# Layer with attention and experts on one core: zeros on ScalarE, the last gate's modulation in the attention stage, another order in the routing

## The chip, the cores and the metric

The kernel runs on one core of a Trainium2 chip. A core has five engines that run their own instruction queues and wait for each other through semaphores: TensorE (PE, matmuls), VectorE (DVE), ScalarE (ACT), GpSimd (POOL) and SyncE (SP, which here issues the large DMA transfers). The metric is the device time of one execution in microseconds.

## The reference

One layer over 512 tokens of width 1024, float32. A conditioning vector c gives six modulations (shift, scale and gate, twice).

```python
cond = silu(c)
mod = cond @ ada_w[l] + ada_b[l]
sh1, sc1, gt1, sh2, sc2, gt2 = split(mod, 6)
h = _ln(x) * (1 + sc1) + sh1
parts = split(h @ w_in[l])                 # one projection, three mixers
y = concat([mla(...), window(...), nsa(...)]) @ w_out[l]
x = layernorm(ALPHA * x + (1 + gt1) * y)
h = _ln(x) * (1 + sc2) + sh2
scores = sigmoid(h @ router_w); biased = scores + router_bias
# pick 1 of 4 groups of experts by its best two, then 2 of its 4 experts;
# weights are the two scores, normalised
g, u = h @ w_gate[e], h @ w_up[e]          # per expert, 1024 -> 256
y = sum over chosen e of weight * ((silu(g) * u) @ w_down[e])
x = layernorm(ALPHA * x + (1 + gt2) * y)
```

`gt2`, the last gate, is needed only at the very end of the expert stage.

## The kernel before, in words

The 512 tokens are four blocks of 128 (n = 0 to 3). The stages in order of time: modulations and input projection; MLA, sliding window and NSA attention by token block, interleaved by hand in the string `ORD` (`q` queries, `n` NSA of a token block, `s` modulation steps, `g` steps of the last gate's modulation, `o` output projection, `Z` and `L` mark where buffers change hands); output projection of a block with its layernorm; routing of that block; experts. The order on each engine comes from a planner that lists instructions by priority, with offsets in the table `PRM` and a few forced places (`issue_after`, `together`).

A modulation step (`mod_half`) loads four weight tiles `ada`, multiplies them with the conditioning vector in 16 matmuls into `modps` (two `gemv` of 8) and adds the result in two VectorE adds. `gstep` is that of gate 2. In the `ORD` of before no `g` stands, so its two steps run where `step(16, gsteps)` is written, after the last output projection, and `gate_out(1, m3)` adds one and writes the gate to DRAM, from where `gate_in` reads it back for all partitions. Weight tiles `ada`, the output weights' `wo20` to `wo31`, the gates and the gather targets `x1g` share five buffers of a pool (`wraw`).

The output weights of the last two parts are split into a high part `woh` (a cast on ScalarE) and a low part `wol` (a subtraction on GpSimd).

Routing (`route(n, ...)`): transposes of the normalized rows (`x1p`, copied to `x1T`), logits `lps`, their sum `lsum`, the router's function `th`, affinities `aff`, biased scores `bia`, group sums `gs`, choice of group and experts (`asg`), ranks by matmuls (`rkp`), one-hot operands (`rh`, `r`, `rg`), and tables by matmuls: `tabp` gives `tokB`, the token indices of the gathers, `tabq` the weights and output places. Then `prep(q)` gathers the rows of an expert group's row blocks (`rows`), block b=0 from the first two token blocks alone (`xsA_d`), b=1 and 2 from all (`xs_d`); they are transposed (`gTp`) and evicted with scale and shift on ScalarE (`gT`). Gathers skip missing rows, so their targets are zeroed first.

Experts: four groups q of four experts. For each group eight steps k of gate/up matmuls (`gu`), each for three row blocks b, then `silu`, product, transposes `atp`, down projection `dn`, and combination. `warm` matmuls of no use to the result keep TensorE's clock up during the routing. The small tables `tokh` and `cmxp` are needed for the output's indices and for a count of overflowing rows.

## Time and profile before

| what | us |
|---|---|
| median of 3 runs | 593.4 (591.91 to 599.62) |
| the profiled execution | 596.7 |
| its span, first to last instruction | 594.8 |
| attention of token blocks 2 and 3, with output projection of blocks 0 and 1 | about 255 to 346 |
| rest of the output projection, routing of blocks 0 to 2 | 346 to 384.6 |
| routing of block 3, first expert block | 384.6 to 427.4 |
| experts, to the end of the span | 427.4 to 594.8 |

Times in the trace count from the start of the span. A row gives an instruction or a run of like ones; "idle before" with an arrow names who ended an engine's wait. The mean granted TensorE clock of the execution was 0.965 of full speed.

### The profile page before, as it was taken

The page shows a single profiled execution, that of the slowest core. Times are in us where ns is not written, and L with a number is a line of the kernel's source. Part 1 is how long each engine was busy: PE and PEld are TensorE (multiplying, and loading weights), DVE is VectorE, ACT ScalarE, POOL GpSimd, SP SyncE. Part 2 cuts the span into 40 slices and gives each one's busy share as a digit, 9 for nine tenths or more (in the row PEclk, how much of TensorE's full clock was granted, in tenths as well). Part 3 has the DMA queues.
Part 4 walks back from the last instruction along what each step waited for, and adds up shares of the span by engine and source line. Part 5 has one row for each costly group of instructions (what it writes and reads, how often), then busy time and mean ns, then how long its engine had stood idle before and what let it go on. Part 6 is the DMA issues. An engine that isn't in the chain of part 4 may idle for free.

```text
span 594.8 us, 10444 instructions
## 1 busy us (share of the span) xinstructions
PE 548.7 (92%) x3856; PEld 333.1 (56%) x3856; DVE 368.2 (62%) x1219; ACT 222.1 (37%) x556; POOL 97.4 (16%) x114
## 2 busy tenths in 40 slices
PE   2899999999899999999899999978899999999990
PEld 1559775687788998755455456653434234234240
DVE  7515656664678568877769568886138157167174
ACT  2514443561428336374634512121434062070130
POOL 0114200000010010003301112123502122011022
PEclk9969999999799999999999999978999999999996
DMA  8993246743930200098300685359699999999601
GB/s 301 373 328 108 83 142 225 260 153 102 323 91 19 72 37 1 2 220 226 124 2 0 222 278 200 119 209 306 164 370 351 366 365 348 374 356 354 248 1 47
DMA packets 77546, 117.05 MB, mean 197 GB/s; under 512 B 7937, under 2 KB 54440, under 8 KB 77492
## 3 DMA queue, kind: packets, MB, share of 16 engines
q1 hardware_dynamic: 72328, 102.60, 52.9%
q0 software_dynamic: 4960, 13.64, 6.3%
q8 instruction: 32, 0.52, 0.4%
q14 instruction: 22, 0.18, 0.1%
q10 hardware_dynamic: 204, 0.11, 0.1%
HBM read 112.12 MB, written 8.40 MB: 203 GB/s over the span
## 4 chain that ended last, share of the span: by engine, by line
PE 78%; DVE 11%; issue 3%; DMA 3%; ACT 2%; POOL 2%; ACTq 0%; POOLq 0%
PE gu L1319 13%; PE zps L407 13%; PE dn L1370 7%; PE onsa L894 6%; PE yps L1215 5%; PE zall L423 3%; PE modps L323 2%; PE modps L375 2%; PE gTp L997 2%; PE cmb L1410 2%; PE stp L501 2%; PE sps L921 2%; PE wps L849 1%; PE warm L356 1%; PE cmh L1418 1%
## 5 line engine op out<-in xcount | busy, mean ns | idle before, releaser
L1319 PE MATMUL gu<-gu,gT 128*32 128x512 f32 x768 | 85.3, 596 | 0.1
L1319 PEld LDWEIGHTS gu<-gu,gT 128*32 128x32 f32 x768 | 23.8, 110 | 52.5 <-issue 50.6
L1370 PE MATMUL dn<-dn,aT 128*32 128x512 f32 x384 | 45.3, 597 | 0.4 <-ACT aT L127 0.2
L1343 DVE TENSOR_TENSOR act<-act,gu 128x256 f32<-128x256 f32 x12 | 5.1, 421 | 59.8 <-ACT act L1342 59.8
L1002 ACT ACTIVATE gT<-gTp,modc,modc 128x128 f32<-128x128 f32 x96 | 35.7, 461 | 10.1 <-PE gTp L997 9.5
L1342 ACT ACTIVATE act<-gu 128x256 f32<-128x256 f32 x12 | 4.6, 387 | 72.1 <-PE gu L1319 72.1
L1215 PE MATMUL yps<-wol,oM 128*128 128x512 f32 x64 | 30.9, 595 | 0.0
L1375 DVE SCALAR_TENSOR_TENSOR y<-dn,tab,gt 128x512 f32<-128x512 f32 x24 | 18.0, 748 | 10.2 <-PE dn L1370 10.2
L323 PE MATMUL modps<-ada,cond 128*32 128x512 f32 x128 | 18.3, 631 | 4.4 <-DVE gr L1079 4.1
L1370 PEld LDWEIGHTS dn<-dn,aT 128*32 128x32 f32 x384 | 10.4, 109 | 20.8 <-issue 18.5
L894 PE MATMUL onsa<-pt,vs 128*64 128x512 f32 x40 | 20.6, 614 | 0.0
L491 ACT ACTIVATE Sg<-Sg,nms 128x128 f32<-128x128 f32 (+3 forms) x32 | 17.8, 559 | 3.7 <-DVE nms L490 3.3
L491 ACT ACTIVATE W<-W,nmw 128x256 f32<-128x256 f32 (+1 forms) x32 | 15.3, 478 | 9.7 <-DVE nmw L490 9.3
L997 PEld LDWEIGHTS gTp<-cf,rows 128*128 128x128 f32 x96 | 10.4, 142 | 15.1 <-ACT gT L1002 9.2
L448 DVE TENSOR_TENSOR rp<-zps,trig 128x128 f32<-128x128 f32 (+1 forms) x28 | 9.7, 345 | 12.9 <-PE zps L407 12.5
L356 PE MATMUL warm<-cf 128*128 128x128 f32 x88 | 17.2, 326 | 0.1
L407 PE MATMUL zps<-B1s,hH 128*128 128x256 f32 x64 | 15.1, 329 | 2.2 <-DVE B1s L210 1.1
L356 PEld LDWEIGHTS warm<-cf 128*128 128x128 f32 x88 | 13.8, 222 | 5.5 <-issue 4.7
L1378 DVE TENSOR_TENSOR ys<-y,ys 128x512 fp32r<-128x512 f32 x22 | 15.2, 692 | 2.1 <-ACT ys L127 1.4
L997 PE MATMUL gTp<-cf,rows 128*128 128x128 f32 x96 | 14.8, 282 | 1.6 <-DMA rows<-xs_d,tokB 1.6
L127 ACT COPY pt<-stp 128x512 f32<-128x512 f32 x14 | 7.9, 586 | 22.2 <-PE stp L501 21.9
L1389 ACT ACTIVATE R<-R,rsf 128x1024 f32<-128x1024 f32 x3 | 3.7, 1241 | 31.4 <-DVE rsf L1388 31.4
...
## 6 DMA issues: line engine op xcount, KB each, us to landing
...
```

The costliest lines, as they stand in the source:

```text
L323: return lambda: PE.matmul(ps[32 * j:32 * j + 32], cond[:, k], t[:, 512 * (j % 2):512 * (j % 2) + 512], start=first, stop=last, skip_group ...
L356: PE.matmul(ps[:, :128], ident, ident, start=True, stop=True)
L407: PE.matmul(ps[:, :w], l[:, k, ts_], get(k, r), start=(k == 0 and i == 0), stop=(k == KD - 1 and i == 2))
L423: m = PE.matmul(outs[n], l[:, k, n * 128:(n + 1) * 128], get(k, r), start=(beg and n % 2 == 0), stop=(k == KD - 1 and i == 2), skip_group_ ...
L491: S.activation(S_h, S_h, AF.Exp, bias=nm, scale=-1.0, accum_out=den)
L894: PE.matmul(ops[64 * g:64 * g + 64, cols], lhsT, rhs, start=first[g], stop=False, skip_group_check=True)
L997: PE.transpose(ps[:, k * 128:(k + 1) * 128], src[:, (4 * a + k) * 128:(4 * a + k + 1) * 128], ident)
L1002: S.activation(dst[:, kk], pk, AF.Identity, bias=sh2(kk), scale=sc2(kk))
L1215: last = PE.matmul(ps, l, r[:, cs], start=(i == 0), stop=(i == len(order) - 1))
L1319: together([lambda e=e: PE.matmul(gu[b][32 * e:32 * e + 32], gT[b][:, k, 32 * e:32 * e + 32], w[:, e], start=(k == 0), stop=(k == KD - 1), ...
L1370: together([lambda b=b, e=e, f=f: PE.matmul(dn[b][32 * e:32 * e + 32], aT[b][:, f, 32 * e:32 * e + 32], wd[f][:, e], start=(f == 0), stop= ...
L1375: V.scalar_tensor_tensor(y, dn[b], tab[:, s:s + 1], gt2[:, cs], op0=OP.mult, op1=OP.mult)
```

## The change

Four edits. The six buffers that gathers write into (`rows1`, `rows2`, four `x1g`) are zeroed by ScalarE, as a product with zero, instead of GpSimd memsets. The last gate's modulation gets two places `g1` in `ORD`, around the NSA attention of block 2, with priority offset -40. The copies of `x1T` go to ScalarE (which they did) and the pass that writes `t` is listed behind the last of them. The gate/up steps k=3 to 7 of the first expert group are listed behind `tabq` of the last token block.

```diff
@@ -21,9 +21,9 @@
 PRM = {
     "A0": -40, "A1": -300, "A2": 150, "A3": 300, "LA0": -300, "LA1": -40, "LA2": 600, "LA3": -300,
     "NW": [6, 2, 3, 5], "ORA": "k0 k1 k2 l0 l1 l2 l3 k3",
-    "ORD": "q0 q1 n0 n1 q2 q3 s1 n2 Z n3 o0 s2 s1 s2 o1 o2 s2 o3 L", "SWb": 2, "WF": 2, "aTe": "S", "c10": -600,
+    "ORD": "q0 q1 n0 n1 q2 q3 s1 g1 n2 g1 Z n3 o0 o1 o2 o3 L", "SWb": 2, "WF": 2, "aTe": "S", "c10": -600,
     "c11": -40, "c12": -300, "c13": -600, "cpt": "S", "evatp": "S", "evbtp": "SVSV", "evstp": "SSV", "evwtp": "VS",
-    "gst1": 80, "gst2": 40, "kndE": "V", "lTe": "V", "mg": -300, "mh0": 300, "mh2": 20, "mla1": 20, "mla2": 80,
+    "gst1": -40, "kndE": "V", "lTe": "V", "mg": -300, "mh0": 300, "mh2": 20, "mla1": 20, "mla2": 80,
     "mq0": 600, "mq2": 80, "mq3": 150, "mskE": "VG", "mskb": 3, "nl0": 20, "nl1": 150, "nl2": 300, "nl3": 600,
     "np0": -150, "np2": 600, "np3": -80, "ns1": -40, "ns2": 20, "ns3": -40, "nsa1": -20, "nsa3": 600, "nv0": -300,
     "nv1": -20, "nv3": 150, "nw0": 300, "nw1": 600, "nw2": 150, "nw3": -80, "oM": "S", "oNc": "S", "oS": "S",
@@ -39,7 +39,7 @@
     "wB0": 2, "wB1": 3, "wB3": 1, "wK5": 1, "wL3": 2, "wM": 1, "wR0": 4, "wR2": 4, "wR3": 6, "wT2": 2, "wT3": 4,
     "wY31": 4, "wo0": -80, "wo1": 300, "wo2": -300, "wo20": 80, "wo21": -600, "wo3": 150, "wo30": 150,
     "wo31": -600, "woE": "GG", "wohE": "S", "ws0": 4, "ws1": 1, "ws3": 1, "wz0": 1, "wz3": 2, "wzf0": 1,
-    "x1T": "SS", "x1bk": "tq", "ybk": "z", "yhi": "V", "yhi3": "S", "ylo": "V", "ylo3": "VG", "yxb": 4, "zrb": 5,
+    "x1bk": "tq", "ybk": "z", "yhi": "V", "yhi3": "S", "ylo": "V", "ylo3": "VG", "yxb": 4, "zrb": 5,
 }
 T, D, NT, KD = 512, 1024, 4, 8
 NEG = -1.0e30
@@ -937,7 +937,17 @@
                 with pri(f[t[0]][1] + t[1]):
                     f[t[0]][0](int(t[1]))
 
-        outproj = gstep = None
+        gsteps = []
+
+        def gstep(n):
+
+            if not gsteps:
+                step(16)
+                gsteps.extend((mod_bias(10, 2), 0))
+                gsteps[1] = mod_half(gsteps[0], 1)
+            step(n, gsteps[1])
+
+        outproj = None
         ORD = pr("ORD", "q0 n0 q1 n1 s1 q2 q3 Z n2 n3 L o0 o1 o2 g1 o3 g1")
         partA, partB = ORD.split("Z")
         partB, partC = partB.split("L")
@@ -970,12 +980,6 @@
                 load_wo(a, b, wol[a][:, b])
         gt1 = wraw("gt1")
         gate_in(0, gt1)
-        m3 = mod_bias(10, 2)
-        gsteps = mod_half(m3, 1)
-
-        def gstep(n):
-            step(n, gsteps)
-
         for a in range(WF, 4):
             for b in range(2):
                 raw = wraw(f"wo{a}{b}")
@@ -1055,6 +1059,7 @@
             V.memset(g8[n], BIGF)
             V.memset(t8[n], BIGF)
         base = rp.tile([128, 20], F32, name="base")
+        tabq = []
 
         def route(n, lps, rs):
             def r_(name, *shape):
@@ -1162,7 +1167,8 @@
             for kk in range(2):
                 PE.matmul(tq[:, 0:2 * NSLOT], ohp[:, kk], r2[:, kk].rearrange("p a c -> p (a c)"), start=(kk == 0),
                           stop=False, skip_group_check=True)
-            warm(f"wT{n}", PE.matmul(tq[:, 2 * NSLOT:2 * NSLOT + 8], ohg, rg, start=False, stop=True, skip_group_check=True))
+            tabq.append(PE.matmul(tq[:, 2 * NSLOT:2 * NSLOT + 8], ohg, rg, start=False, stop=True, skip_group_check=True))
+            warm(f"wT{n}", tabq[-1])
             V.tensor_tensor(tab[:, NSLOT:], tab[:, NSLOT:], tq[:, 0:TW - NSLOT], op=OP.add)
             if n == NT - 1:
                 V.tensor_copy(tokG, tab[:, 3 * NSLOT:])
@@ -1229,13 +1235,14 @@
                     ps = bank(pick("x1bk", "t", hf), "x1p")
                     for k in range(4):
                         PE.transpose(ps[:, k * 128:(k + 1) * 128], x1[:, (4 * hf + k) * 128:(4 * hf + k + 1) * 128], ident)
-                    cp(pick("x1T", "SS", hf), x1T[:, 4 * hf:4 * hf + 4], heads(ps, 4))
+                    x1c = S.copy(x1T[:, 4 * hf:4 * hf + 4], heads(ps, 4))
                     V.bn_stats(st[:, hf], x1[:, cs])
             G.dma_start(x1_d[n * 128:(n + 1) * 128], x1)
             fin()
             nm = yp.tile([128, 1], F32, name="ynm", bufs=2)
             V.scalar_tensor_tensor(nm, mv2[:, 0:1], -1.0, rs2, op0=OP.mult, op1=OP.mult)
-            S.activation(t2, x1, AF.Identity, bias=nm, scale=rs2)
+            with tc.issue_after(x1c.ins):
+                S.activation(t2, x1, AF.Identity, bias=nm, scale=rs2)
             for d_ in (xsA_d, xs_d)[n >= 2:]:
                 G.dma_start(d_[n * 128:(n + 1) * 128], t2)
 
@@ -1268,11 +1275,15 @@
         ep = pool(est, "ep", 2, side="right")
         wst2 = pool(est, "wst2", NW2, side="right")
         rows_ += [ep.tile([128, D], F32, name=f"rows{i}", bufs=1) for i in range(1, NROW)]
+        def zero(dst):
+
+            S.mul(dst, cf[:, :dst.shape[-1]], 0.0)
+
         for r in rows_[1:]:
-            G.memset(r, 0.0)
+            zero(r)
         cnt_w = [0]
-        step(16, gsteps)
-        gate_out(1, m3)
+        gstep(16)
+        gate_out(1, gsteps[0])
         gt2 = wraw("gt2")
         gate_in(1, gt2)
         lg2 = ep.tile([128, D], F32, name="lg2", bufs=1)
@@ -1315,17 +1326,19 @@
                 for u, nm in enumerate(("moe_w_gate", "moe_w_up")):
                     SP.dma_start(w[:, :, 256 * u:256 * u + 256],
                                  A[nm][4 * q:4 * q + 4, k * 128:(k + 1) * 128].rearrange("e p f -> p e f"))
-                for b in range(CAPB):
-                    together([lambda e=e: PE.matmul(gu[b][32 * e:32 * e + 32], gT[b][:, k, 32 * e:32 * e + 32], w[:, e],
-                                                    start=(k == 0), stop=(k == KD - 1), skip_group_check=True)
-                              for e in range(4)])
+
+                with tc.issue_after(tabq[-1].ins) if q == 0 and k >= 3 else nullcontext():
+                    for b in range(CAPB):
+                        together([lambda e=e: PE.matmul(
+                            gu[b][32 * e:32 * e + 32], gT[b][:, k, 32 * e:32 * e + 32], w[:, e],
+                            start=(k == 0), stop=(k == KD - 1), skip_group_check=True) for e in range(4)])
             if pending:
                 pending.pop()()
             with pri("mg"):
                 x1g, x2g = x1g_[2 * (q % 2)], x1g_[2 * (q % 2) + 1][:, 0:512]
                 if q < 2:
-                    G.memset(x1g, 0.0)
-                    G.memset(x2g, 0.0)
+                    zero(x1g)
+                    zero(x2g)
                 gather(x1g, x1_d[:, :], tokG[:, 2 * q:2 * q + 1], T - 1)
                 if GP > 128:
                     gather(x2g, x1h, tokH[:, q:q + 1], 2 * T - 1)
```

TensorE in the routing of the last token block. `rkp` are the rank matmuls, `gu_k` is the weight tile of gate/up step k (here of the first row block), `tabp` and `tabq` build the tables, `gTp` are the transposes of gathered rows. In the kernel before:

```order
L1096 MATMUL rkp<-base,cf 128x20
L1096 MATMUL rkp<-asg_3530,ones 128x20
L1097 MATMUL rkp<-asg_3531,cf 128x20
L1319 MATMUL gu_4794<-gu_3_4842,gT 32x512 x4
L356 MATMUL warm<-cf 128x128 x5
L1319 MATMUL gu_4794<-gu_4_4857,gT 32x512 x4
L356 MATMUL warm<-cf 128x128
L1319 MATMUL gu_4794<-gu_5_4872,gT 32x512 x4
L1319 MATMUL gu_4794<-gu_6_4887,gT 32x512 x4
L1129 MATMUL tabp<-rh,ohp 128x12 x2
L1163 MATMUL tabq<-r_4626,ohp 128x24 x2
L1165 MATMUL tabq<-rg,ohg 128x8
```

In the changed kernel:

```order
L1101 MATMUL rkp<-base,cf 128x20
L1101 MATMUL rkp<-asg_3568,ones 128x20
L356 MATMUL warm<-cf 128x128 x2
L1102 MATMUL rkp<-asg_3569,cf 128x20
L356 MATMUL warm<-cf 128x128 x6
L1134 MATMUL tabp<-rh,ohp 128x12 x2
L1168 MATMUL tabq<-r_4664,ohp 128x24 x2
L1170 MATMUL tabq<-rg,ohg 128x8
L1332 MATMUL gu_4794<-gu_3_4842,gT 32x512 x4
L1332 MATMUL gu_4794<-gu_4_4857,gT 32x512 x4
L1332 MATMUL gu_4794<-gu_5_4872,gT 32x512 x4
L1332 MATMUL gu_4794<-gu_6_4887,gT 32x512 x4
L1001 MATMUL gTp<-cf,rows_4712 128x128 x8
```

Steps k=3 to 6 stood among the rank matmuls and ahead of `tabp`; now they stand behind the last `tabq`, and step k=7 and the small matmuls `tokh` and `cmxp` come after the transposes `gTp`.

TensorE around the gate-2 modulation `modps` (its weight tiles are `ada_01` to `ada_71`). In the kernel before it stands at the start of the last token block's routing, `yps` being the last matmuls of the output projection:

```order
L1215 MATMUL yps<-wol_3454,oh_4433 128x512
L1215 MATMUL yps<-woh_3450,ol_4434 128x512
L1096 MATMUL rkp<-base,cf 128x20
L323 MATMUL modps_4678<-ada_11_4681,cond 32x512
L323 MATMUL modps_4678<-ada_01_4679,cond 32x512 x2
L323 MATMUL modps_4678<-ada_11_4681,cond 32x512
L323 MATMUL modps_4678<-ada_31_4689,cond 32x512
L323 MATMUL modps_4678<-ada_21_4687,cond 32x512 x2
L323 MATMUL modps_4678<-ada_31_4689,cond 32x512
L323 MATMUL modps_4697<-ada_51_4700,cond 32x512
L323 MATMUL modps_4697<-ada_41_4698,cond 32x512 x2
L323 MATMUL modps_4697<-ada_51_4700,cond 32x512
```

In the changed kernel its second half stands in the attention of token blocks 2 and 3 (`sps` scores, `onsa` values, `wtp` transposes of the window branch), the first half some twenty us of work before that:

```order
L471 MATMUL qntp_3606<-cf_87,qr_3099 128x128 x4
L921 MATMUL sps_3426<-ksS1_399,qn1H_3217 128x384
L921 MATMUL sps_3426<-ksS1_399,qn1L_3218 128x384
L894 MATMUL onsa_2891<-pt_3023,vs_402 64x512
L323 MATMUL modps2_3463<-ada2_51_3466,cond_160 32x512
L323 MATMUL modps2_3463<-ada2_41_3464,cond_160 32x512 x2
L323 MATMUL modps2_3463<-ada2_51_3466,cond_160 32x512
L1221 MATMUL yps_3883<-wol0_3492,oM0_406 128x512
L323 MATMUL modps2_3463<-ada2_71_3474,cond_160 32x512
L323 MATMUL modps2_3463<-ada2_61_3472,cond_160 32x512 x2
L323 MATMUL modps2_3463<-ada2_71_3474,cond_160 32x512
L1221 MATMUL yps_3883<-wol0_3492,oM0_406 128x512
```

All four pieces moved there; the output-projection matmuls `yps`, which fill TensorE's queue in the attention stage, now begin among the last of them.

GpSimd in the routing of the last token block (`rows` and `x1g` are targets of gathers). In the kernel before:

```order
L1289 DMA rows0_4662<-xsA_d_64,tokA_3523 128x1024
L1272 MEMSET rows1_4674 128x1024
L1272 MEMSET rows2_4675 128x1024
L1327 MEMSET x1g0_4722 128x1024
L1328 MEMSET x1g1_4723 128x512
L1327 MEMSET x1g2_4724 128x1024
L1328 MEMSET x1g3_4725 128x512
L1289 DMA rows1_4674<-xs_d_63,tokB_3524 128x1024
```

ScalarE at the same place in the changed kernel (`x1T` copies for the router, `t` normalized rows, `gT` evictions of the transposes, `th` the router's function):

```order
L1280 ACTIVATE x1g_4725<-cf 128x512
L1238 COPY x1T<-x1p 128x512 x2
L1245 ACTIVATE t_4470<-yt,ynm,yrs_4528 128x1024
L1006 ACTIVATE gT<-gTp,modc_1513,modc_3537 128x128 x8
L1280 ACTIVATE rows_4712<-cf 128x1024
L1280 ACTIVATE rows_4713<-cf 128x1024
L1073 ACTIVATE th<-lg 128x16
L1006 ACTIVATE gT<-gTp,modc_1513,modc_3537 128x128 x8
L1355 ACT_TABLE_LOAD
```

The memsets are gone from GpSimd; three ScalarE passes of six are seen here, the other three stand in the attention stage. The `x1T` copies stand ahead of `t`, and the table load stands behind the second eight `gT`.

## Rows read from the trace of the kernel before

**Rows 1.** From the page, the busy time of each engine over the whole span (share of the span, number of instructions).

```profile
PE 548.7 (92%) x3856; PEld 333.1 (56%) x3856; DVE 368.2 (62%) x1219; ACT 222.1 (37%) x556; POOL 97.4 (16%) x114
```

**Rows 2.** Busy time by stretches of the span: start and end, length, then the busy us of TensorE (PE), its weight loads, VectorE (DVE), ScalarE (ACT) and GpSimd (POOL) with instruction counts, the granted TensorE clock, the DMA engines' busy share and GB/s.

```profile
261.90:289.00 27.10, 27.10 (x141) 15.08 (x140) 20.44 (x91) 16.79 (x46) 8.24 (x4) 1.00 0.76 200
289.00:306.40 17.40, 15.84 (x59) 6.98 (x58) 10.60 (x25) 7.07 (x15) 2.36 (x1) 1.00 0.21 63
...
346.40:358.00 11.60, 10.70 (x52) 6.40 (x52) 9.59 (x34) 1.32 (x3) 1.83 (x3) 1.00 1.06 352
358.00:384.60 26.60, 25.88 (x148) 17.93 (x148) 22.09 (x118) 5.79 (x9) 6.91 (x10) 1.00 0.40 137
384.60:401.70 17.10, 13.03 (x98) 8.34 (x99) 14.78 (x70) 4.61 (x10) 3.37 (x5) 0.80 0.60 223
401.70:416.20 14.50, 11.77 (x82) 5.38 (x80) 9.75 (x51) 2.09 (x4) 4.98 (x7) 0.88 0.97 311
```

**Rows 3.** The chain of work that ended last, in order of time: start, us, what held the chain. From the routing of the last token block, and one piece from the dense expert stage (second expert group).

```profile
403.07 0.89 POOL rows L1272
...
406.68 10.89 issue
...
417.79 4.25 DMA rows<-xs_d,tokB
...
459.22 20.74 PE gu L1319 x192
```

**Rows 4.** Timeline, VectorE and GpSimd: `aff` of token block 2 (384.17) and of block 3 (402.63), the first and the last memsets, and the group sum `gs` of block 3. Columns: start, us, engine, line, operation, out<-in, shape, count, and in brackets the idle time before it and what ended that.

```profile
384.17 0.17 DVE L1142 TENSOR_SCALAR aff<-th 128x16 f32<-128x16 f32 x1
...
402.10 1.86 POOL L1272 MEMSET rows<- 128x1024 f32 x2
...
402.63 4.08 DVE L1142 TENSOR_SCALAR aff<-th 128x16 f32<-128x16 f32 x1
...
406.14 0.54 POOL L1328 MEMSET x1g<- 128x512 f32 x1
...
406.76 0.18 DVE L1076 TENSOR_REDUCE gs<-pr 128x4 f32<-128x24 f32 x1
```

**Rows 5.** Timeline, from the last rank matmul of block 3 to the transposes of its gathered rows: TensorE, and the one-hot table operand `rh` on VectorE.

```profile
408.76 0.40 PE L1097 MATMUL rkp<-asg,cf 128*128 128x20 f32 x2 [2.73 <-DVE asg L1088]
...
410.18 2.50 PE L356 MATMUL warm<-cf 128*128 128x128 f32 x10
...
411.57 0.23 DVE L1126 TENSOR_SCALAR rh<-oht,cf 128x24 f32<-128x24 f32 x1
...
416.21 0.61 PE L1129 MATMUL tabp<-rh,ohp 128*128 128x12 f32 x4
...
417.77 0.30 PEld L1171 LDWEIGHTS tokh<-tab,cf 128*128 128x128 f32 x2
...
419.43 1.06 PE L1319 MATMUL gu<-gu,gT 128*32 128x512 f32 x8
...
422.09 1.09 PE L997 MATMUL gTp<-cf,rows 128*128 128x128 f32 x8 [1.59 <-DMA rows<-xs_d,tokB]
```

**Rows 6.** Timeline, the modulation of gate 2 where it stands in this kernel: its matmuls `modps` on TensorE and two of its adds on VectorE, then the router's logits `lps` and their sum `lsum` of block 3.

```profile
384.63 1.92 PE L323 MATMUL modps<-ada,cond 128*32 128x512 f32 x16
...
386.78 0.67 DVE L548 TENSOR_TENSOR mod<-modps,mod 64x512 f32<-64x512 f32 x1
...
387.63 0.69 DVE L548 TENSOR_TENSOR mod<-modps,mod 64x512 f32<-64x512 f32 x1
...
390.63 1.94 PE L323 MATMUL modps<-ada,cond 128*32 128x512 f32 x8 [4.07 <-DVE gr L1079]
...
396.38 1.06 PE L323 MATMUL modps<-ada,cond 128*32 128x512 f32 x8
...
399.58 0.64 PE L1244 MATMUL lps<-x1T,rwc 128*32 128x128 f32 x16
...
401.69 0.29 PE L1251 MATMUL lsum<-cf,x1T 128*128 128x16 f32 x2
```

**Rows 7.** Two stretches of the routing, columns as in rows 2; the granted TensorE clock is the third number from the end.

```profile
390.00:396.00 6.00, 5.37 (x25) 3.73 (x26) 5.41 (x38) 1.98 (x3) 1.59 (x3) 0.50 0.62 250
...
408.00:414.00 6.00, 5.24 (x29) 2.92 (x29) 4.21 (x37) 0.00 (x0) 0.00 (x0) 0.72 1.06 375
```

**Rows 8.** Timeline, GpSimd's `wol` subtractions and VectorE beside them: `sc` of an earlier token block (246.93, no subtraction near) and of block 2 (278.95), the scaling of `Sg`, and TensorE's transposes `stp` of it.

```profile
246.93 0.28 DVE L865 TENSOR_TENSOR sc<-sc,dc 128x128 f32<-128x128 f32 x1
...
275.73 4.68 POOL L985 TENSOR_TENSOR wol<-wo,woh 128x1024 fp32r<-128x1024 f32 x2 [14.28 <-DMA lb<-in_ln_b_dram]
...
278.95 1.61 DVE L865 TENSOR_TENSOR sc<-sc,dc 128x128 f32<-128x128 f32 x1
...
289.67 3.24 DVE L133 TENSOR_SCALAR Sg<-Sg,dns 128x384 f32<-128x384 f32 x3
...
290.00 2.36 POOL L985 TENSOR_TENSOR wol<-wo,woh 128x1024 fp32r<-128x1024 f32 x1 [4.03 <-ACT woh L127]
...
292.64 1.20 PE L501 MATMUL stp<-cf,Sg 128*128 128x128 f32 x7 [1.56 <-DVE Sg L133]
```

**Rows 9.** Timeline, ScalarE: the 1024-column pass that writes the normalized rows `t` of block 3, and its load of the function table for the experts.

```profile
394.02 1.24 ACT L1238 ACTIVATE t<-yt,ynm,yrs 128x1024 f32<-128x1024 f32 x1 [10.19 <-DVE key L1099]
...
402.53 1.28 ACT L1342 ACT_TABLE_LOAD   x1
```

## The prediction

> **What bounds the kernel now.** I read the table of busy time first: TensorE is busy for 548.7 of 594.8 us [rows 1], so most of the span is its work, and a gain must come from a stretch where it stands idle. The table by stretches finds them [rows 2]: 261.9 to 289 us (attention, token blocks 2 and 3) is full, 27.10 of 27.10; 358 to 384.6 (output projection) nearly, 25.88 of 26.60; 384.6 to 401.7 holds 13.03 of 17.10, 401.7 to 416.2 holds 11.77 of 14.50. After 427.4 the experts run without waits; one group's 192 gate/up matmuls take 20.74 us in one piece [rows 3]. So what counts is when the dense expert stage begins, and that hangs on one chain: router logits of the last token block, their decision on VectorE, the tables on TensorE, the gather on GpSimd, transposes of the gathered rows. The chain of waits shows where it is held [rows 3]: the memsets on GpSimd (403.07 to 406.68), 10.89 us of "issue" in which GpSimd waits for its index, 4.25 us of gather.
>
> **The change, part by part.** The sum is made against the profiled execution, 596.7 us, of which the span is 594.8; the median of the runs shown is 593.4, so the profiled one is 3.3 us longer, and I carry the difference over to the median.
>
> *Zeros.* Six memsets leave GpSimd. In the trace the small VectorE operation `aff` takes 4.08 us at 402.63 and ends when the last memset ends (406.14 + 0.54); for the block before it took 0.17 us [rows 4]. `gs` behind it starts at 406.76; without the hold it would start at about 403.0 (0.17 for `aff` and three overlapping adds, 0.1 apart). Gain: **3.8 us** on the chain. ScalarE pays instead: four passes of 1024 columns, each bounded by the 1.24 us of `t` over the same width [rows 9], and two of 512 at half that, about 6.2 us. Three stand in the attention stage, one in the routing of block 2, two after block 0's eight `gT` and before the last `th`. Those two (2.5 us) are covered if `gT` ends 2.5 us before `lsum`; `gT`'s transposes now stand ahead of the modulation's old place, so I take nothing, and 1 us if that cover fails.
> The Trainium skill (SBUF — State Buffer, "Who interferes with whom") says VectorE and GpSimd share a pair of ports that whoever issues first holds for one whole instruction. By that, `aff` should get in when the memset under way ended, near 403.07, and the gain would be 0.3 us instead of 3.8; here it waited through five more, so the row decides.
>
> *First expert block behind the tables.* In the row of before, the last block's table matmul `tabp` begins at 416.21, though its input `rh` was ready at 411.80 [rows 5]: TensorE's queue holds gate/up steps k=4, 5, 6 and warm-ups before it. Now only warm-ups stand there. Those warm-ups (12 matmuls at the 0.25 us of the row at 410.18) behind the last rank matmul (408.76) reach to about 412.2, so `tabp` starts there by the old times: **4.0 us** sooner, and `tokB`, the gather and the rows with it. Do the displaced steps then hold the transposes? From `tabp` to `gTp` were 5.88 us (416.21 to 422.09). The tables take up to 1.56 (416.21 to 417.77, a warm-up included) and four steps at 1.06 take 4.2: 5.8, still just shorter. At the lower clock a step takes 1.9 (the 8 matmuls at 390.63 [rows 6]), giving 9.3 and a loss of 3.4: that is one bound.
> The price: step k=7 (1.06 us) and the small `tokh`, `cmxp` and warm-up matmuls (417.77 to 419.43, 1.66 us) stood in the wait for the gather, for nothing. Now they stand behind the transposes, in a stage without waits. Cost: 1.06 + 1.66, **2.7 us**. ScalarE's load of a function table (1.28 us at 402.53 [rows 9]) goes from idle time to between two blocks' `gT`; gate/up steps of block 1 cover it, or it costs up to 1.
>
> *Gate-2 modulation out of the routing.* 32 matmuls of 1.92, 1.94 and 1.06 us per piece and the adds (0.67, 0.69) go [rows 6]. Until 390.6 they filled a wait for the layernorm, so the first two pieces bought nothing but a warm clock. The adds at 386.78 and 387.63 sit between this block's statistics and its normalization, so up to 1.3 us of the layernorm goes. Against it `lps` (399.58) now has steps k=0 and 1 ahead, and `lsum` (401.69) k=2, 1.0 to 1.9 us each. The granted clock is 0.50 from 390 to 396 [rows 7], which is the lower of its two levels (1.2 of 2.4 GHz), after an idle stretch of 4.07 us; with the modulation gone TensorE is idle longer there. I take **0**, bounds -1.2 and +1.6. On SyncE four loads and the gate's write leave the queue in front of the last expert weights; those are not waited for in before, so nothing. Forcing the `x1T` copies ahead of the `t` pass gives the router its operand 1.24 us earlier, but `lps` stands behind TensorE's own queue: nothing.
>
> *The modulation in the attention stage.* 32 matmuls at full clock, 4 x 0.96 = 3.84 us, come into 255 to 283 us. That stretch is full by virtue of output-projection matmuls that fill it; they move to later and meet the idle there (1.56 in 289 to 306.4, 0.90 in 346.4 to 358, 0.72 in 358 to 384.6 [rows 2]), but I doubt that waits on other engines get filled exactly. At worst all 3.84 us stay and 2.4 us are added where VectorE (20.44 of 27.10 busy, and 2.4 us of adds more) paces a stretch without fillers. Bounds 0 and 6.2. Eight loads come earlier on SyncE and the output weights `wo20` to `wo31` wait for the buffers they free. That reorders their split into high and low parts: four subtractions on GpSimd, in before two at 275.73 (4.68 us), one later and one at 290.00 (2.36). Beside them VectorE was held twice: `sc` took 1.61 instead of 0.28, and three scalings of `Sg` 3.24, for which TensorE waited 1.56 [rows 8]. In the new order the casts that feed them stand behind the `Sg` scalings, so that wait should go; others (the gate's own add of 1, copies of `pt` behind it) may come. I take **+2.7** for the whole part.
>
> *Sum:* -3.8 - 4.0 + 2.7 + 0 + 2.7 = **-2.4 us**: 594.3 against 596.7, or 591 against the median of 593.4. Two per cent is 11.9 us, about what a measurement of this kernel can tell from no change.
>
> **The rivals.**
> *A, the attention stage takes the modulation for nothing.* For it: those 3.2 us of idle time on TensorE later, and the `Sg` wait that goes. Against: the waits there end on VectorE, so filler work helps only if it stands right before them. Then the routing's -5.1 stands alone, with the layernorm's 1.2 perhaps -6.3: 587.
>
> *B, slower: the subtractions on GpSimd hold VectorE where TensorE waits for it.* In the new order all four stand in a row behind the mask of block 2, and on VectorE the gate's add of 1 and then copies of `pt` for `onsa` come at about that time. The price is that of two subtractions in one run, 4.68 us (the row at 275.73, beside which the short `sc` was held to the end), on top of 6.2 for the unfilled stretch; against the routing's -5.1 that is +5.8: 599. It decides if the first cast comes before VectorE has taken the gate's add. Against it: the casts are spaced by copies that themselves need VectorE's results, which breaks the run.
>
> *C, the hold was for one memset only.* If the memsets' hold ends after the instruction under way, and `aff` was late for another reason, zeros give 0.3 (403.07, where the second memset begins in the chain [rows 3], less 402.8) instead of 3.8, and the sum is +1.1: 594.5. This is what the page named above gives; five memsets passed during `aff`, which speaks against it.
>
> *D, the clock.* With less TensorE work before 397 the lower level lasts through steps k=0 to 2, or the two idle stretches after `lsum` bring it in steps k=3 to 6: +1.6 and +3.4 at most, so 593 to 596. For it: the 0.72 at 408 to 414 [rows 7].
>
> *E, the change doesn't do what it says:* the table matmuls stay late, since the chain is held by warm-ups or `lsum` and not by steps. Then the 4.0 fall away and the price stays, -3.8 + 2.7 + 2.7: 595.
>
> **How the numbers follow.** Forecast (588 to 594) 0.42, A 0.20, B 0.12, C 0.06, D 0.12, E 0.03, and 0.05 for a gain over 2% that I can't derive. A and the forecast's lower side reach to 584 if VectorE's relief and A come together; the range leaves out B's upper half and takes 584 to 598. No case comes to -11.9: both routing gains in full, -7.8, the layernorm's -1.2 and a free attention stage give -9.0 before the price of 2.7. Slower by over 2% needs B at twice its price, a third of B: 0.04; within 2% stay 0.91.
>
> **What would show it.** `aff` of the last block at about 0.2 us, with no memset beside it; `tabp` within half a microsecond of `rh`, before steps k=3 to 6; a gather wait in front of `gTp` of block 1 under 1 us; the uninterrupted gate/up piece starting at about 425 instead of 427.4, of which 2.7 is the attention stage's; the end of the output projection at about 387 instead of 384.6. The prediction is wrong if that end comes before 385.5 (then A), after 390 (then B), or if the granted clock between 396 and 416 stays at 0.5.

## The result and the profile after

The changed kernel takes 601.0 us (median of 20 runs, of which one took 1207 us and is left out of the ratio) against 594.6 us for the kernel before on the same chips: ratio 1.011, 95% interval [1.008, 1.013]. That is slower, by 6.4 us or 1.1%, and outside the predicted range of 584 to 598. The profiled execution took 603.7 us, its span is 601.9 us.

Busy time hardly moved. From the page of the changed kernel, first table (busy us, share of the span, instructions):

```profile
PE 551.1 (92%) x3856; PEld 334.0 (55%) x3856; DVE 363.3 (60%) x1219; ACT 227.4 (38%) x562; POOL 92.5 (15%) x108
```

Against [rows 1], ScalarE took up the zeros (+5.3) and GpSimd gave them away (-4.9); TensorE has 2.4 us more, with the same 3856 instructions; that some of them ran at a lower clock is seen further down.

To see where the time went, I cut the span at events that both traces have: the last matmul of the input projection (`zps`, 250.8 before, 248.5 after), the sums of the router's weights `rsum` (L1033 of the changed kernel), the last output-projection matmul `yps`, the last block's table `tabp`, the transposes `gTp` of gathered block 1, and the uninterrupted piece of 192 `gu` matmuls of the second expert group [rows 3]. The first two stretches are called attention and output projection for short. But `rsum` is only a mark amid the attention of blocks 2 and 3, whose last matmul `onsa` ends at 346.5 before and 354.6 after; so the second stretch holds the rest of the attention too, and the two are best read together. Lengths in us:

| from, to | before | after | difference | predicted |
|---|---|---|---|---|
| `zps` to `rsum` (attention, first part) | 55.4 | 64.6 | +9.2 | +2.7 for both |
| `rsum` to last `yps` (rest of attention, output projection) | 78.3 | 81.9 | +3.6 | |
| `yps` to `tabp` (routing) | 31.6 | 24.6 | -7.0 | -7.8 |
| `tabp` to `gTp` (gather) | 5.9 | 7.1 | +1.3 | 0 |
| `gTp` to the 192-matmul piece | 37.1 | 39.5 | +2.4 | +2.7 |
| sum | 208.4 | 217.8 | +9.5 | -2.4 |

The stretch ahead of `zps` was 2.4 us shorter in this execution; nothing of the change stands there, and in the other runs below it ends anywhere from 245.2 to 251.5. The piece itself and all behind it take 135.7 us in both. So the routing came close to its forecast (partly by luck, as the experiments will show), and the attention stage did not.

Busy time by stretches of the changed kernel, columns as in [rows 2]; the first stretch of the table runs from 248.5 to 313, the routing of the last block from 395:

```profile
262.00:272.00 10.00, 9.57 (x53) 5.49 (x51) 7.03 (x40) 6.95 (x25) 0.00 (x0) 1.00 1.05 321
272.00:279.00 7.00, 3.46 (x9) 1.21 (x9) 6.64 (x32) 1.37 (x3) 1.20 (x1) 0.67 0.39 155
279.00:287.20 8.20, 8.16 (x25) 4.85 (x25) 4.81 (x19) 5.33 (x15) 0.00 (x0) 0.65 0.00 1
287.20:291.30 4.10, 4.10 (x22) 1.10 (x22) 3.40 (x10) 1.36 (x6) 0.00 (x0) 1.00 0.39 106
...
394.80:412.00 17.20, 12.44 (x83) 8.25 (x81) 12.12 (x66) 7.82 (x14) 3.67 (x5) 0.70 1.01 334
412.00:422.00 10.00, 7.00 (x50) 6.39 (x50) 6.34 (x53) 0.22 (x1) 0.39 (x1) 0.79 0.01 2
422.00:431.88 9.88, 9.88 (x76) 3.35 (x76) 1.49 (x6) 4.39 (x10) 5.19 (x8) 0.87 0.65 197
```

The second line is the one to look at. Where [rows 2] had 27.10 of 27.10 us busy at full clock, TensorE now stands idle half the time (3.46 of 7.00) while VectorE is full (6.64), and there and behind it the granted clock is 0.67 and 0.65, so the next 8.16 us of "busy" are in good part work at the lower of the two levels (1.2 of 2.4 GHz). The timeline of TensorE there (start, us, instruction, and in brackets the idle time before it and its cause):

```profile
272.91 0.66 PE L501 MATMUL stp<-cf,Sg 128*128 128x128 f32 x4 [1.13 <-ACT pt L127]
275.52 1.97 PE L894 MATMUL onsa<-pt,vs 128*64 128x512 f32 x2 [1.96 <-DVE pt L127]
277.42 0.90 PE L501 MATMUL stp<-cf,Sg 128*128 128x128 f32 x3
279.04 0.69 PE L921 MATMUL sps<-ksS,qn0H 128*128 128x384 f32 x1 [0.72 <-DVE nms L490]
...
286.24 1.07 PE L894 MATMUL onsa<-pt,vs 128*64 128x512 f32 x2
287.24 1.07 PE L323 MATMUL modps<-ada,cond 128*32 128x512 f32 x8
288.24 1.12 PE L1221 MATMUL yps<-wol,oM 128*128 128x512 f32 x2
289.29 1.06 PE L323 MATMUL modps<-ada,cond 128*32 128x512 f32 x8
```

Three waits for small operations on ScalarE and VectorE (1.13, 1.96, 0.72) stand open, and two `onsa` matmuls take 1.97 us at 275.52, where the same pair takes 1.07 at 286.24. In the kernel before the first output-projection matmuls `yps` ran at 261.95 and filled such gaps:

```profile
261.95 1.02 PE L1215 MATMUL yps<-wol,oM 128*128 128x512 f32 x2
```

In the changed kernel the first `yps` comes at 288.24, right behind a piece of the moved modulation.

The routing of the last block in the changed kernel (VectorE, TensorE, GpSimd, ScalarE):

```profile
414.04 0.17 DVE L1147 TENSOR_SCALAR aff<-th 128x16 f32<-128x16 f32 x1
...
416.52 0.40 PE L1102 MATMUL rkp<-asg,cf 128*128 128x20 f32 x2 [2.14 <-DVE asg L1093]
...
419.33 0.23 DVE L1131 TENSOR_SCALAR rh<-oht,cf 128x24 f32<-128x24 f32 x1
...
419.62 1.03 PE L1134 MATMUL tabp<-rh,ohp 128*128 128x12 f32 x4 [0.86 <-DVE rh L1131]
...
421.85 4.98 PE L1332 MATMUL gu<-gu,gT 128*32 128x512 f32 x32
...
426.76 1.09 PE L1001 MATMUL gTp<-cf,rows 128*128 128x128 f32 x8
...
430.37 1.28 ACT L1355 ACT_TABLE_LOAD   x1
```

`aff` takes 0.17 us instead of 4.08 [rows 4], and `tabp` follows `rh` by 0.06 us where 4.4 us lay between them before [rows 5]: both as forecast. The tables (1.03 us each, 0.61 in [rows 5]) and the four gate/up steps (4.98 us, four times 1.06 by [rows 5]) ran partly at the lower level of the clock; 0.79 was granted in the stretch from 412 to 422, in which TensorE had stood idle for 3 us.

### The profile page after: what moved, and what is told of

It is laid out like the page before. It is cut to its first block, busy times and chain, and to the rows that moved or that the text cites. A ratio compares the mean times of both kernels' runs of the same rounds, so it can differ in the third digit from the quotient of the medians.

```text
span 601.9 us, 10449 instructions
## 1 busy us (share of the span) xinstructions
PE 551.1 (92%) x3856; PEld 334.0 (55%) x3856; DVE 363.3 (60%) x1219; ACT 227.4 (38%) x562; POOL 92.5 (15%) x108
## 4 chain that ended last, share of the span: by engine, by line
PE 80%; DVE 11%; DMA 4%; ACT 2%; issue 2%; POOL 1%; ACTq 0%; POOLq 0%; DVEq 0%
PE gu L1332 14%; PE zps L407 12%; PE dn L1383 7%; PE yps L1221 7%; PE onsa L894 5%; PE zall L423 3%; PE modps L323 2%; PE gTp L1001 2%; PE cmb L1423 2%; PE modps L375 2%; DMA ada<-in_ada_w_dram 2%; PE sps L921 2%; PE warm L356 2%; PE wps L849 2%; PE stp L501 1%
## 5 line engine op out<-in xcount | busy, mean ns | idle before, releaser
L1332 PEld LDWEIGHTS gu<-gu,gT 128*32 128x32 f32 x768 | 24.4, 112 | 55.9 <-issue 51.4
L1221 PE MATMUL yps<-wol,oM 128*128 128x512 f32 x64 | 32.2, 606 | 0.0
L1383 PEld LDWEIGHTS dn<-dn,aT 128*32 128x32 f32 x384 | 10.4, 109 | 20.3 <-issue 17.9
L1001 PEld LDWEIGHTS gTp<-cf,rows 128*128 128x128 f32 x96 | 11.3, 149 | 11.7 <-ACT gT L1006 9.2
L1221 PEld LDWEIGHTS yps<-wol,oM 128*128 128x128 f32 x64 | 11.0, 191 | 8.2 <-issue 7.5
L501 PEld LDWEIGHTS stp<-cf,Sg 128*128 128x128 f32 x80 | 9.3, 144 | 11.2 <-issue 8.8
```

What stands on the lines that cost most here:

```text
L1001: PE.transpose(ps[:, k * 128:(k + 1) * 128], src[:, (4 * a + k) * 128:(4 * a + k + 1) * 128], ident)
L1221: last = PE.matmul(ps, l, r[:, cs], start=(i == 0), stop=(i == len(order) - 1))
L1332: together([lambda e=e: PE.matmul(gu[b][32 * e:32 * e + 32], gT[b][:, k, 32 * e:32 * e + 32], w[:, e], start=(k == 0), stop=(k == KD - 1), ...
L1383: together([lambda b=b, e=e, f=f: PE.matmul(dn[b][32 * e:32 * e + 32], aT[b][:, f, 32 * e:32 * e + 32], wd[f][:, e], start=(f == 0), stop= ...
```

## The experiments

The question was what cost 12.8 us in attention and output projection where I had put 2.7. The theories at the start: *F*, the fillers: modulation and `yps` take the same pair of PSUM buffers in program order, so with the modulation's second half late in the queue no filler can come before it. *B* (my rival; the expectations call it S): GpSimd's subtractions hold VectorE. *O* in the expectations: the loss lies elsewhere, in the zeros on ScalarE or the order of the `x1T` copies. And the clock as a follower of any of them. The changed kernel was edited back in parts, then the kernel before was given the parts one by one. All lengths are cut at the events of the first table, in one profiled execution each; median and ratio are of 8 to 12 runs (20 for "after"), the ratio against the kernel before on the same chip (medians 594.6 to 595.8 us), with its 95% interval.

| kernel | attention | output proj. | routing | gather | to 192-piece | sum | median us | ratio |
|---|---|---|---|---|---|---|---|---|
| before | 55.4 | 78.3 | 31.6 | 5.9 | 37.1 | 208.4 | 594.6 | 1 |
| after | 64.6 | 81.9 | 24.6 | 7.1 | 39.5 | 217.8 | 601.0 | 1.011 [1.008, 1.013] |
| e1_gate_back | 55.4 | 78.3 | 24.9 | 10.8 | 41.2 | 210.6 | 599.4 | 1.006 [1.003, 1.009] |
| e2_gate_only | 63.6 | 81.5 | 25.6 | 6.0 | 37.1 | 213.8 | 597.9 | 1.006 [1.001, 1.010] |
| e6_g_pri | 57.1 | 76.7 | 22.1 | 5.9 | 39.5 | 201.4 | 590.7 | 0.992 [0.989, 0.995] |
| e4_g_late | 55.9 | 80.1 | 24.2 | 8.6 | 39.6 | 208.4 | 592.5 | 0.996 [0.992, 0.999] |
| f5_bank_q | 55.1 | 78.8 | 24.5 | 7.1 | 39.5 | 205.0 | 592.5 | 0.994 [0.991, 0.998] |
| e5_g_both_late | 55.4 | 83.1 | 21.2 | 6.0 | 39.5 | 205.3 | 594.4 | 0.997 [0.994, 1.001] |
| f1_k_free | 57.0 | 76.7 | 26.0 | 5.9 | 37.1 | 202.8 | 589.1 | 0.991 [0.988, 0.995] |
| f2_zero_pool | 57.0 | 76.9 | 24.9 | 5.9 | 39.5 | 204.2 | 591.1 | 0.995 [0.991, 0.998] |
| g1_zero_only | 55.4 | 78.3 | 26.4 | 10.7 | 38.6 | 209.4 | 593.9 | 0.999 [0.995, 1.002] |
| g2_k_only | 55.4 | 78.3 | 26.9 | 10.4 | 40.9 | 211.9 | 595.6 | 1.001 [0.998, 1.004] |
| g3_gate300 | 57.0 | 77.1 | 26.5 | 5.9 | 37.1 | 203.6 | 589.8 | 0.990 [0.987, 0.993] |
| g4_f1_bank_q | 62.2 | 74.0 | 26.0 | 5.9 | 38.8 | 206.9 | 591.2 | 0.993 [0.990, 0.997] |

The runs of one kernel lie up to 9.7 us apart, so differences under about 3 us between medians are not read as differences below. The difference in the column "sum" (one execution) and that of the medians agree within 4 us for every kernel.

### e1_gate_back: the changed kernel with the modulation back in the routing

```diff
-    "ORD": "q0 q1 n0 n1 q2 q3 s1 g1 n2 g1 Z n3 o0 o1 o2 o3 L", "SWb": 2, "WF": 2, "aTe": "S", "c10": -600,
+    "ORD": "q0 q1 n0 n1 q2 q3 s1 n2 Z n3 o0 o1 o2 o3 L", "SWb": 2, "WF": 2, "aTe": "S", "c10": -600,
-    "gst1": -40, "kndE": "V", ...
+    "kndE": "V", ...
```

> The changed kernel with the two g1 taken out of ORD, so the gate-2 modulation stands in the routing again; zeros on ScalarE, the x1T order and steps k=3 to 7 behind the tables stay. Theory F (fillers: the modulation's place costs 12.5 us of the changed trace, because the output-projection matmuls that filled TensorE's queue between 255 and 285 us could not start before it): the attention stage is as before (end of the output projection at 384 to 385 us), only the routing's gain of about 3 to 5 us is left: 590 to 592 against a median of 594.6. Theory S (GpSimd's subtractions hold VectorE): the same, since they move back too. Theory O (the loss is elsewhere, in the zeros on ScalarE or the order of the x1T copies): still slower than before, 597 to 601.

Measured 599.4 us, which by the total is theory O's range and not F's 590 to 592. The stretches say otherwise: attention and output projection are as before to 0.1 us, so all of the +12.8 belongs to the modulation's move. But the two routing edits, with the `x1T` order beside them, did not bring 5 us either: routing -6.7, gather +4.9, price +4.1. (The profiled execution, 595.3 us, was the shortest of twelve; the others are taken up at the end.) The timeline of e1: SyncE's queue, the gather (GpSimd) and the transposes that wait for it:

```profile
397.47 0.51 SPq L345 DMA_DIRECT2D gt_d<-mod  x1
398.04 0.39 SPq L1327 DMA_DIRECT2D gu<-in_moe_w_gate_dram  x1
...
400.37 0.65 SPq L1327 DMA_DIRECT2D gu<-in_moe_w_up_dram  x1
...
408.03 1.02 POOL L1300 DMA_INDIRECT rows<-xs_d,tokB  x1 [9.46 <-issue]
...
417.20 1.09 PE L1001 MATMUL gTp<-cf,rows 128*128 128x128 f32 x8 [4.01 <-DMA rows<-xs_d,tokB]
```

And the stretch around the gather's issue (columns as in [rows 2], the DMA engines' share is the last but one):

```profile
403.00:410.00 7.00, 5.37 (x36) 3.50 (x40) 5.25 (x40) 0.68 (x2) 1.67 (x2) 0.86 1.07 379
```

From the gather's issue to the transposes are 9.2 us, not the 4.25 of [rows 3]. The DMA engines are full there (1.07): the gate's write `gt_d` stands in SyncE's queue behind the late modulation, the last expert weights behind it, and the layer-norm vectors behind those. In the kernel before the gather was issued only at 417.8, when that traffic was over. This was a second theory (*G*): an earlier table is worth nothing as long as the gather then meets the weights.

### e2_gate_only: the kernel before with the modulation's move alone

```diff
-    "ORD": "q0 q1 n0 n1 q2 q3 s1 n2 Z n3 o0 s2 s1 s2 o1 o2 s2 o3 L", "SWb": 2, "WF": 2, "aTe": "S", "c10": -600,
+    "ORD": "q0 q1 n0 n1 q2 q3 s1 g1 n2 g1 Z n3 o0 o1 o2 o3 L", "SWb": 2, "WF": 2, "aTe": "S", "c10": -600,
-    "gst1": 80, "gst2": 40, "kndE": "V", ...
+    "gst1": -40, "kndE": "V", ...
...
+            if not gsteps:
+                step(16)
+                gsteps.extend((mod_bias(10, 2), 0))
+                gsteps[1] = mod_half(gsteps[0], 1)
+            step(n, gsteps[1])
```

> The kernel before with the gate-2 modulation alone moved into the attention stage (g1 n2 g1, offset -40). Theory F: the loss of the attention stage without the routing's gain, but the routing loses its modulation matmuls: 9 to 13 us slower than before, 604 to 607. Theory S: the same. Theory O: 594 to 597.

Measured 597.9 us: slower, as expected, but by less than the 604 to 607 of theory F. Attention and output projection lose 11.3 us, and the routing gains 6.0 with the zeros still on GpSimd and the steps' order not forced. So the move by itself brings the gain for which the other two edits were priced. Rows of GpSimd, VectorE and TensorE show how (e2):

```profile
406.29 1.86 POOL L1276 MEMSET rows<- 128x1024 f32 x2
...
413.32 0.17 DVE L1146 TENSOR_SCALAR aff<-th 128x16 f32<-128x16 f32 x1
...
419.14 0.23 DVE L1130 TENSOR_SCALAR rh<-oht,cf 128x24 f32<-128x24 f32 x1
...
419.43 0.61 PE L1133 MATMUL tabp<-rh,ohp 128*128 128x12 f32 x4
```

Two memsets are left here (the four of `x1g` now stand before the routing); they end five microseconds before `aff` and hold nothing. And `tabp` follows `rh` by 0.06 us, without the order that was to bring this.

### e6_g_pri: the changed kernel with another priority of the modulation

```diff
-    "gst1": -40, "kndE": "V", ...
+    "gst1": 300, "kndE": "V", ...
```

> The changed kernel with the offset of the g steps at 300 instead of -40: the second half of the modulation then stands on TensorE near row 1054 instead of 1107, and the output-projection matmuls begin at row 1083 instead of 1110; the work is the same and the four subtractions on GpSimd still stand in a row. Theory F: half or more of the attention stage's 9 us comes back, 594 to 597. Theory S: the subtractions still hold VectorE, 600 to 602. A third theory, that TensorE's own 3.84 us and the modulation's adds cost their full time wherever they stand in this stage: 598 to 600.

Measured 590.7 us, better than theory F had put it (594 to 597). One number takes the 12.8 us away (attention 57.1, output projection 76.7, together 133.8 against 133.7 before). e6's stretches and its TensorE rows:

```profile
262.00:272.00 10.00, 10.00 (x63) 6.22 (x63) 7.70 (x37) 6.23 (x21) 0.00 (x0) 1.00 1.05 250
272.00:279.00 7.00, 7.00 (x30) 3.14 (x28) 5.53 (x23) 0.90 (x2) 0.00 (x0) 1.00 1.03 246
279.00:287.00 8.00, 8.00 (x44) 3.83 (x44) 5.93 (x23) 5.85 (x15) 1.23 (x2) 1.00 0.77 225
```

```profile
259.84 1.06 PE L323 MATMUL modps<-ada,cond 128*32 128x512 f32 x8
...
264.68 1.06 PE L323 MATMUL modps<-ada,cond 128*32 128x512 f32 x8
...
268.90 1.02 PE L1221 MATMUL yps<-wol,oM 128*128 128x512 f32 x2
```

The last two pieces of the modulation run at 259.84 and 264.68 instead of 287.24 and 289.29; `yps` follows at 268.90, and 272 to 279 is full at full clock. The four subtractions on GpSimd run from 286.98 on here (9.6 us in all), and in the changed kernel from 295.42 on, behind the stretch that lost the time; so rival B falls.

### f5_bank_q: another PSUM buffer for the modulation's half, priority left at -40

```diff
-                ps = bank("z", "modps2")
+                ps = bank("q" if a else "z", "modps2")
```

> The changed kernel with one thing other: the gate-2 modulation's sums stand in PSUM bank q (one buffer) instead of z (two buffers, which the output projection's sums take too). The modulation's matmuls stay where they are on TensorE (rows 1028 to 1039 and 1103 to 1120), but the output-projection matmuls now begin at row 1070 instead of 1110. Theory F in the form that the z buffers kept the fillers behind the modulation: the empty stretch of TensorE between 272 and 284 us and its lower clock go, 591 to 596 against 601. If the place of the modulation itself is what costs (its matmuls, its loads, its adds): 599 to 602.

Measured 592.5 us, attention 55.1. This edit leaves the modulation late and takes away only the shared buffer; f5's rows on TensorE, and the stretch that stood half idle in the changed kernel:

```profile
267.20 1.02 PE L1221 MATMUL yps<-wol,oM 128*128 128x512 f32 x2
...
280.28 1.06 PE L323 MATMUL modps<-ada,cond 128*32 128x512 f32 x8
```

```profile
272.00:279.00 7.00, 7.00 (x26) 2.75 (x24) 4.60 (x19) 1.79 (x5) 0.00 (x0) 1.00 0.07 25
```

The filler now passes the modulation. That is theory F's own test: place and cost of the modulation are about the same, the lock is gone, and so is nearly all of the loss. (Not quite all: in f5 the 16 `modps` matmuls of another modulation step, 1.9 us, stand ahead of the cut at `zps`, behind it in the other kernels but g4. With them attention and output projection take 135.8 us, 2.1 more than before, where the changed kernel takes 146.5.)

### e4_g_late and e5_g_both_late: the modulation later, behind the first output projection

```diff
-    "ORD": "q0 q1 n0 n1 q2 q3 s1 g1 n2 g1 Z n3 o0 o1 o2 o3 L", "SWb": 2, "WF": 2, "aTe": "S", "c10": -600,
+    "ORD": "q0 q1 n0 n1 q2 q3 s1 g1 n2 Z n3 o0 g1 o1 o2 o3 L", "SWb": 2, "WF": 2, "aTe": "S", "c10": -600,
```

> The changed kernel with the second g1 behind o0 instead of ahead of Z: fillers begin at row 1054 on TensorE, as in the kernel before (1049), and the second half of the modulation at row 1171. Theory F: the attention stage costs 2 to 4 us more than before instead of 9, the routing keeps its gain: 592 to 596. Theory S: subtractions are still behind the mask of block 2 in one row, 599 to 602.

```diff
-    "ORD": "q0 q1 n0 n1 q2 q3 s1 g1 n2 g1 Z n3 o0 o1 o2 o3 L", "SWb": 2, "WF": 2, "aTe": "S", "c10": -600,
+    "ORD": "q0 q1 n0 n1 q2 q3 s1 n2 Z n3 o0 g1 o1 g1 o2 o3 L", "SWb": 2, "WF": 2, "aTe": "S", "c10": -600,
```

> The changed kernel with both g1 in the output projection (n2 Z n3 o0 g1 o1 g1 o2): fillers begin at row 1049 as in the kernel before, the modulation's matmuls stand among those of the output projection (rows 1168 to 1267) and its loads no longer stand beside the routing's gather. Theory F: attention as before, 4 x 0.96 us more in the output projection, the routing's gain in full: 588 to 593. If the gather is held by loads as it was with the modulation in the routing (9.2 us from issue to transposes there): 595 to 600.

Measured 592.5 and 594.4 us, the second just above theory F's 588 to 593. The moved pieces run at 310.9 and 312.6 in e4, at 308.1, 321.2 and 348.8 in e5. Attention is back at 55.9 and 55.4 in both; the output projection grows by 1.8 and 4.8 (e5 has both halves there). e4 also shows the clock (rival D of the prediction) at its largest in the gather's stretch:

```profile
411.70:420.40 8.70, 8.66 (x43) 3.62 (x43) 2.32 (x11) 0.00 (x0) 4.59 (x7) 0.54 0.44 124
```

Its four gate/up steps before `gTp` take 6.47 us there, and 3.64 in e6, at full clock: 2.8 us in the gather's stretch.

### f1_k_free and f2_zero_pool: e6 without the steps' order, e6 without ScalarE's zeros

```diff
-                with tc.issue_after(tabq[-1].ins) if q == 0 and k >= 3 else nullcontext():
+                with nullcontext():
```

> The kernel with the g steps' offset at 300 (590.7 median), with steps k=3 to 7 of the first expert block free again to stand ahead of the tables. By the prediction's terms (4.0 gained at the tables, 2.7 paid behind them) this loses 1.3 us: 591.5 to 593. If the price is paid in any case, it loses 4: 594 to 595. If the order at this place is worth nothing: 590 to 591.

```diff
-            S.mul(dst, cf[:, :dst.shape[-1]], 0.0)
+            G.memset(dst, 0.0)
```

> The kernel with the g steps' offset at 300 (590.7 median), with the zeros as GpSimd memsets again. Three of the six now stand early (behind the four subtractions) and three at the routing, of which two (1.9 us in a row) right behind the first gather. If VectorE is held as long as memsets run, aff of the last block takes up to 2 us and the kernel 591 to 593; if the hold in the kernel before came from the row of six, nothing: 590 to 591. The prediction's 3.8 us in full would give 594.5.

Measured 589.1 and 591.1 us, both like e6 (590.7). With the modulation early, neither of the two edits is worth anything that these runs can tell. In f1 the tables come 3.8 us later than in e6 and the price of 2.4 us is not paid. In f2 the last memsets run at 395.58 to 397.44 and `aff` at 401.46, undisturbed.

### g1_zero_only and g2_k_only: one routing edit alone on the kernel before

```diff
-            G.memset(r, 0.0)
+            zero(r)
...
-                    G.memset(x1g, 0.0)
-                    G.memset(x2g, 0.0)
+                    zero(x1g)
+                    zero(x2g)
```

> The kernel before with the zeros alone on ScalarE. The prediction's term: aff of the last block from 4.08 to 0.2 us, and 3.8 us of it reach the end: 591 against 595. Theory G (the gather of the last block's rows then leaves while the last expert weights, which the late gate holds back, still fill the DMA engines, as in the run with the gate's modulation in the routing, where it took 9.2 us): aff is short, but the gather lands where it did, 594 to 598.

```diff
...
+                with tc.issue_after(tabq[-1].ins) if q == 0 and k >= 3 else nullcontext():
...
```

> The kernel before with steps k=3 to 7 of the first expert block behind the tables and nothing else. The prediction's terms: 4.0 gained, 2.7 paid, 593 to 594 against 595. Theory G: the tables come 4 us sooner, the gather waits for the weights in the DMA engines, and the price behind it is paid: 596 to 599.

Measured 593.9 and 595.6 us, both no change. The rows of g1:

```profile
399.62 0.17 DVE L1142 TENSOR_SCALAR aff<-th 128x16 f32<-128x16 f32 x1
...
408.21 1.02 POOL L1293 DMA_INDIRECT rows<-xs_d,tokB  x1 [10.90 <-issue]
...
417.30 1.97 PE L997 MATMUL gTp<-cf,rows 128*128 128x128 f32 x8 [6.38 <-DMA rows<-xs_d,tokB]
```

And of g2:

```profile
396.02 1.86 POOL L1274 MEMSET rows<- 128x1024 f32 x2
...
396.55 4.08 DVE L1143 TENSOR_SCALAR aff<-th 128x16 f32<-128x16 f32 x1
...
400.05 0.55 POOL L1332 MEMSET x1g<- 128x512 f32 x1
...
407.77 1.03 POOL L1291 DMA_INDIRECT rows<-xs_d,tokB  x1 [7.17 <-issue]
```

Both do what I had forecast for them up to the table (routing -5.3 and -4.8 us), and both lose it in the gather (+4.8 and +4.5), which takes 9.1 and 8.4 us from issue to transposes. This shows theory G on the kernel before itself: the gate's modulation, not the table, decided when the rows could land, since SyncE's last weights stood behind it.

### g3_gate300 and g4_f1_bank_q: looking for the best

g3 is the kernel before with the modulation moved early and nothing else, that is e2 with

```diff
-    "gst1": -40, "kndE": "V", ...
+    "gst1": 300, "kndE": "V", ...
```

> The kernel before with the gate-2 modulation alone moved (g1 n2 g1), at offset 300 so that the fillers are not held. Theory F with G: attention and output projection cost about nothing (as in the run at 300: -0.1), the routing loses its modulation matmuls and the late weights, 589 to 593. If zeros and order are what helps the runs at 300: 594 to 596.

g4 is f1 with f5's buffer:

```diff
-                ps = bank("z", "modps2")
+                ps = bank("q" if a else "z", "modps2")
```

> Offset 300, PSUM bank q for the modulation's sums, zeros on ScalarE, steps k=3 to 7 free: the fillers begin at row 1078 with no modulation behind them that holds a z buffer. Theory F: attention as short as with bank q (55.1 us from the last projection matmul to rsum, against 57.0 at offset 300 with bank z), 587 to 589. If the filling was already complete: as the run with free steps, 589 to 590.

g3: 589.8 us, 0.990 [0.987, 0.993]; with f1 (589.1) the fastest seen, and faster than both kernels. Its gather is undisturbed. The timeline of g3 (zeroed rows, `aff`, gather, transposes):

```profile
393.54 1.86 POOL L1276 MEMSET rows<- 128x1024 f32 x2
...
402.16 0.17 DVE L1146 TENSOR_SCALAR aff<-th 128x16 f32<-128x16 f32 x1
...
409.85 1.03 POOL L1293 DMA_INDIRECT rows<-xs_d,tokB  x1 [14.46 <-DVE tab L1170]
...
414.18 1.09 PE L1001 MATMUL gTp<-cf,rows 128*128 128x128 f32 x8 [1.62 <-DMA rows<-xs_d,tokB]
```

And the same stretch as in e1:

```profile
403.00:410.00 7.00, 6.93 (x60) 4.39 (x58) 5.74 (x47) 0.34 (x1) 0.15 (x1) 1.00 0.00 0
```

The DMA engines stand idle from 403 to 410 (1.07 in e1), since SyncE has issued the last weights by 384; the gather takes 4.3 us. g3 against f1 also tells of the fourth edit, the `x1T` copies ahead of `t`: f1 has it and the zeros on ScalarE beside the early gate, g3 has neither, and they differ by 0.7 us.

g4 missed its expectation: the other buffer brought nothing on top of the early place (attention 62.2, output projection 74.0, together 136.2 against f1's 133.7; `rsum` itself comes later in the queue there, so only the sum compares). With the 1.9 us that stand ahead of the cut, as in f5, it is 4.4 us longer than f1, and the 55.1 against 57.0 on which the expectation rested was itself this shift of the cut. In g4's trace `yps` has run ahead to weights that GpSimd has not split yet:

```profile
288.16 0.50 PE L1221 MATMUL yps<-wol,oh 128*128 128x512 f32 x1 [1.08 <-POOL wol L989]
...
298.93 0.50 PE L1221 MATMUL yps<-wol,oh 128*128 128x512 f32 x1 [0.77 <-POOL wol L989]
```

f1 has no such wait there. Whether these waits make up the difference I did not test.

## Why the prediction was wrong

**The failed step is the term "the modulation in the attention stage", +2.7 with bounds 0 and 6.2; it measured +12.8** (e2: +11.3, without the other edits). I had written that the filling `yps` "move to later and meet the idle there", and took only what the added 3.84 us of matmuls and 2.4 of adds could cost. The stretch that was full "by virtue of output-projection matmuls" lost them altogether until 288 us, since their PSUM buffers come behind the modulation's in the queue. I had shown that order myself: in the changed kernel `yps` begins among the last `modps`. I read it as a shift, and did not ask what keeps `yps` from coming earlier. f5 answers it: with another buffer `yps` passes the modulation, and 10.7 of the 12.8 us are gone. In the trace of after the attention's +9.2 are 3.9 us more idle time on TensorE (5.7 against 1.8), the modulation's 3.8, and some 4.0 for matmuls at the lower level of the clock, less six of the thirty `yps` that moved out (10.09 us of them against 12.71), which the output projection then has to do. (The 4.0 is an estimate: at a mean of 0.65 the lower level holds for seven tenths of the time, so 8.16 x 0.7 / 2, and 3.46 x 0.66 / 2 for the stretch before it.) So also the sign "end of the output projection at about 387" was off: 395.0, past the 390 that I had named for rival B. But B's mechanism is not the cause (e6).

**The clock** was in the prediction only as rival D, in the routing. It did act there (0.79 in 412 to 422, gather's stretch +1.3, below the most that D allowed, 3.4), but most of it lay in the attention stage, where I had no term for it.

**Zeros:** -3.8 forecast; the ranks come 3.65 us sooner behind `lsum` in the changed kernel, and `aff` is 0.17. Right in that trace. The Trainium skill (SBUF — State Buffer, "Who interferes with whom") would end the hold with one GpSimd instruction; g2 repeats the 4.08 us of [rows 4] across six memsets, so the measurement decides, and rival C is out.

**First expert block behind the tables:** -4.0 forecast, -4.35 measured from the ranks to `tabp`; the price 2.7 forecast, 2.4 measured (f1, without the order, does not pay it). Sizes right.

**Gate-2 modulation out of the routing:** forecast 0, bounds -1.2 and +1.6. This was the second wrong step, hidden by the first. Moved alone it gives -6.0 in the routing and behind it (e2: 68.7 us from the last `yps` to the 192-piece, 74.7 before; after: 71.3). The trace of before had the reason: on SyncE "four loads and the gate's write leave the queue in front of the last expert weights", which I priced at nothing because nothing waits for those weights in before. What they delay is the gather, once it is early. Nor did I ask what else the move rearranges: in e2 four of the six memsets leave the routing and `tabp` stands right behind `rh`, the two gains that I had priced elsewhere. So the three terms are no sum: zeros and order alone are worth nothing on the kernel before (g1, g2; both together, with the `x1T` order, were slower: e1), the early gate alone gives all of it, and on top of that the other two cost 2.6 us in the changed kernel's trace (71.3 against 68.7) and nothing measurable where the fillers are free (f1, f2). That the routing's -7.0 came out near the -7.8 of zeros and order is therefore partly luck: without the early gate, which I had put at 0, their gain is lost in the gather (+4.9 in e1), and without them the gate brings -6.0.

**Rival A** (attention for nothing, 587) was wrong for the change as made and right for its neighbour: with the modulation at priority 300 the stage costs nothing, and 589 to 591 us are measured.
